# A zero-padded last product and two later starts in the attention heads of a hybrid decoder layer

## The chip, the cores and the metric

The kernel runs on one core of one Trainium2 chip. The metric is the device time of one execution in microseconds (us), as the median of several runs. TensorE is called PE in the views of the profile (PEld is its weight loads), VectorE DVE, ScalarE ACT, GpSimd POOL, SyncE SP.

## The reference, cut to what matters

One decoder layer on 512 tokens with 16 learned meta tokens ahead of them (L = 528), width 2048. A combined input projection gives q, k, v for 8 heads of 128 columns and the operands of a short convolution; after both groups come an output projection and a SwiGLU feed-forward part. The change lies in the attention heads:

```
q = rmsnorm(q per head, g_q);  k = rmsnorm(k per head, g_k)
z = q k^T / sqrt(128)
log_keep = where(key < query, log_sigmoid(-z), 0)
log_pass = reverse cumulative sum of log_keep over the keys - log_keep
w = where(key < query, exp(log_sigmoid(z) + log_pass), 0)
o = w v
```

Keys are taken in blocks of 128: four whole blocks and a last one of 16 keys (positions 512 to 527), which only the last 16 queries see, so that their weights are a 16 x 16 triangle.

## The kernel before

Activations are kept transposed, with channels on the 128 partitions and tokens along the columns. Products in float32 are made of three products of split operands (hi times hi, hi times lo, lo times hi); ACT casts the hi part and DVE subtracts it for the lo part, for weights (`split_quad`, L188 and L189, into `s_buf`) and for activations (`split`, L300 and L301) alike. The small products of the last two key blocks are plain float32, and the trace shows two PE instructions for each of them.

Each head has three large products of 16 k tiles each: pk, pq and pv. A k tile is six matmuls of 264 columns for pk and pv, and three of 512 columns for pq. The attention of a head is put in between the k tiles of the products that come after, by a list written out by hand: `after(n, work)` issues `work` when n more k tiles have been issued (`tick`). For a head h from 1 to 6 the order on PE is:

- pk of head h: nothing of its own; 8 k tiles later (in pq) the sums of squares of k (`ss_k`, L475 and L476, in `finish` of `qk_norm`).
- pq of head h; 9 k tiles later (in pv) the sums of squares of q (`ss_q`). ACT takes the squares and a scaled copy out of pq (L467, L468), splits the squares (`sh_q`, `sl_q`), and only then can L475 and L476 run.
- pv of head h; 6 k tiles later, in pk of head h+1, `attend`: v's transposes (`va`, `vb`, L522, L523), `v32` (v of the last 128 + 16 keys in plain float32), the scores z (L537 to L543), then softplus terms on ACT, DVE and POOL.
- 14 k tiles later (k tile 4 of pq of head h+1) `sums(2)`, the cumulative sums over the last keys (L592 to L595); 6 k tiles later (10 of pq) `sums(1)`; 6 later (16 of pq, its last) `sums(0)` (both L597 and L598). From the result of one, row 0 of the next one's operand is made: L603 on DVE, then a split on ACT and DVE into `sph` and `spl`. Each also takes its sums off `lb` (L606), takes the exponential (L607), sets what lies past the diagonal to zero on POOL (`causal`, L555), and splits the weights into `wh` and `wl`.
- 11 k tiles after `sums(0)` (k tile 11 of pv) `mix`, the product with v: nine split matmuls (L622 to L624), then L625 for 128 keys and L626 for the last 16. Its result is scaled and split into `st_a` (L629, L630), stored by a DMA on POOL's queue (L446), and its squares are added on POOL.

In heads 0 and 7 the distances are others already: 7 between the sums, and 12 for q in head 0. The scheduler keeps this order on PE. On ACT and DVE the instructions stand in the queue in which the scheduler put them, and each engine runs its own in order. In L626 both operands have 16 partitions, `v32[:16, P:]` and `lw[:16, 1328:1344]`; L543, the score of the same 16 keys, is a product of 128 partitions, 16 columns wide, because `kn` is padded with zeros to 640 columns. After `causal`, columns 1328 to 1343 of `lw` are zero in partitions 16 to 127 too.

Of the kernel before, what the change touches and what calls it, by code (L numbers as in the profile page):

```python
# [9 lines left out]
F32 = mybir.dt.float32  # L10
# [5 lines left out]
P = 128  # L16
D = 2048
SEQ = 512
# [15 lines left out]
def hybrid_layer(ctx: ExitStack, tc: tile.TileContext, xT, w_in, w_out, w_gu, w_down, vecs, out):  # L34
# [373 lines left out]
    kns = [apool.tile([P, 640], F32, name=f"kn{i}") for i in range(1)]  # L408
    for t in kns:
        gp.memset(t[:, L:640], 0.0)  # L410
    acc_c = accpool.tile([P, SEQ], F32, name="acc_c")
    acc_a = accpool.tile([P, SEQ], F32, name="acc_a")

# [76 lines left out]
    def head(h):  # L490

        if h:
            pk = pp.tile([P, 2, 512], F32, tag="pp", name=f"pk{h}")
            product([(pk[:, 0, :H], 0, H), (pk[:, 1, :H], H, L)], n_hl)
        else:
            pk = pk0
        kn = kns[0]
        kh = apool.tile([P, 384], F32R, tag="kh", name=f"kh{h}")
        kl = apool.tile([P, 384], F32R, tag="kl", name=f"kl{h}")
        after(8 if h else 11, qk_norm(halves(pk, H), g_k, L, kn[:, :L], (kh, kl, 384), f"k{h}"))  # L500

        if h:
            pq = pp.tile([P, 2, 512], F32, tag="pp", name=f"pq{h}")
            product([(pq[:, 0, :], META, L)], n_hl)
        else:
            pq = pq0
        qn = apool.tile([P, SEQ], F32, tag="qn", name=f"qn{h}")
        qh = apool.tile([P, SEQ], F32R, tag="qh", name=f"qh{h}")
        ql = apool.tile([P, SEQ], F32R, tag="ql", name=f"ql{h}")
        after(9 if h else 12, qk_norm(pq[:, 0, :], gq_s, SEQ, qn, (qh, ql, SEQ), f"q{h}"))  # L510

        pv = pp.tile([P, 2, 512], F32, tag="pp", name=f"pv{h}")
        product([(pv[:, 0, :H], 0, H), (pv[:, 1, :H], H, L)], n_hl)
        vt = t512(L, "e", 2)
        ve.tensor_tensor(two(vt[:, :L]), halves(pv, H), two(r), ALU.mult)
        after(6 if h else 12, lambda: attend(h, kn, kh, kl, qn, qh, ql, vt))

    def attend(h, kn, kh, kl, qn, qh, ql, vt):

        ta, tb = small(f"va{h}"), small(f"vb{h}")  # L520
        for b in range(4):
            pe.transpose(ta[:, b * P : (b + 1) * P], vt[:, b * P : (b + 1) * P], ident)  # L522
        pe.transpose(tb[:16, :P], vt[:, 512:L], ident)  # L523
        vh = apool.tile([P, 384], F32R, tag="vh", name=f"vh{h}")
        vl = apool.tile([P, 384], F32R, tag="vl", name=f"vl{h}")
        v32 = apool.tile([P, 256], F32, tag="v32", name=f"v32{h}")
        split(vh, vl, ta[:, :384])
        ve.tensor_copy(v32[:, :P], ta[:, 384:512])
        ve.tensor_copy(v32[:16, P:], tb[:16, :P])


        zs = []
        for b in range(3):
            z = small(f"z{h}_{b}")
            kk, q0 = slice(b * P, (b + 1) * P), Q0[b]
            n = SEQ - q0
            pe.matmul(z[:, :n], kh[:, kk], qh[:, q0:], start=True, stop=False)  # L537
            pe.matmul(z[:, :n], kh[:, kk], ql[:, q0:], start=False, stop=False)
            pe.matmul(z[:, :n], kl[:, kk], qh[:, q0:], start=False, stop=True)
            zs.append(z)  # L540
        z = zs[2]
        pe.matmul(z[:, 272:416], kn[:, 384:512], qn[:, 368:], start=True, stop=True)
        pe.matmul(z[:, 416:432], kn[:, 512:640], qn[:, 496:], start=True, stop=True)  # L543


        lw = apool.tile([P, 1344], F32, tag="lw", name=f"lw{h}")
        sp = apool.tile([P, 1344], F32, tag="sp", name=f"sp{h}")
        lb = apool.tile([P, 1344], F32, tag="lb", name=f"lb{h}")

        def causal(t, s):  # L550

            regions = {0: [(0, 112, 16)], 1: [(0, P, 0)], 2: [(0, P, 0), (272, 400, 0), (416, 432, 0)]}
            for a, b, base in regions[s]:
                v = t[:, SEG[s][0] + a : SEG[s][0] + b]
                gp.affine_select(  # L555
                    out=v, in_=v, pattern=[[1, b - a]], compare_op=ALU.is_gt, fill=0.0,
                    base=base, channel_multiplier=-1,
                )

        hl, ws = [None] * 3, [None] * 3  # L560
        for s in (2, 1, 0):
            a, b = SEG[s]
            z = zs[s][:, : b - a]
            sc.activation(lw[:, a:b], z, AF.Abs)
            sc.activation(lw[:, a:b], lw[:, a:b], AF.Exp, scale=-1.0)
            sc.activation(lw[:, a:b], lw[:, a:b], AF.Ln, bias=one[:, 0:1])
            ve.scalar_tensor_tensor(sp[:, a:b], z, 0.0, lw[:, a:b], ALU.max, ALU.add)
            ve.scalar_tensor_tensor(lb[:, a:b], z, 0.0, lw[:, a:b], ALU.min, ALU.subtract)
            causal(sp, s)
            th = apool.tile([P, b - a], F32R, tag=f"th{s}", name=f"sph{h}_{s}")  # L570
            tl = apool.tile([P, b - a], F32R, tag=f"tl{s}", name=f"spl{h}_{s}")
            split(th, tl, sp[:, a:b])
            hl[s] = (th, tl)
            if s == 2:

                late = lw[:, a : a + 288]
                ve.tensor_copy(late[:, :P], sp[:, 1184:1312])
                ve.tensor_tensor(late[:, P:144], sp[:, 1312:1328], sp[:, 1328:1344], ALU.add)
                gp.memset(late[:, 144:272], 0.0)
                ve.tensor_copy(late[:, 272:], sp[:, 1328:1344])  # L580
                bh = apool.tile([P, 288], F32R, tag="bh", name=f"bh{h}")
                bl = apool.tile([P, 288], F32R, tag="bl", name=f"bl{h}")
                split(bh, bl, late)
            else:
                gp.memset(lw[0:1, a : a + Q0[s + 1] - Q0[s]], 0.0)

        def sums(s):
            a, b = SEG[s]
            th, tl = hl[s]
            c = small(f"c{h}_{s}")  # L590
            if s == 2:
                pe.matmul(c[:, :432], later_r, th, start=True, stop=False)  # L592
                pe.matmul(c[:, :432], later_r, tl, start=False, stop=False)
                pe.matmul(c[:, P:416], ones_r, bh, start=False, stop=False)
                pe.matmul(c[:, P:416], ones_r, bl, start=False, stop=True)  # L595
            else:
                pe.matmul(c[:, : b - a], carry, th, start=True, stop=False)  # L597
                pe.matmul(c[:, : b - a], carry, tl, start=False, stop=True)  # L598
            if s:

                n, (a0, b0) = SEQ - Q0[s], SEG[s - 1]
                th, tl = hl[s - 1]
                ve.tensor_tensor(lw[0:1, b0 - n : b0], c[0:1, :n], sp[0:1, a : a + n], ALU.add)  # L603
                split(th[0:1, :], tl[0:1, :], lw[0:1, a0:b0])
                after(6 if 0 < h < HEADS - 1 else 7, lambda: sums(s - 1))
            ve.tensor_tensor(lb[:, a:b], lb[:, a:b], c[:, : b - a], ALU.subtract)  # L606
            sc.activation(lw[:, a:b], lb[:, a:b], AF.Exp)  # L607
            causal(lw, s)
            n = (512, 400, 272)[s]
            th = apool.tile([P, b - a], F32R, tag=f"th{s}", name=f"wh{h}_{s}")  # L610
            tl = apool.tile([P, b - a], F32R, tag=f"tl{s}", name=f"wl{h}_{s}")
            split(th[:, :n], tl[:, :n], lw[:, a : a + n])
            ws[s] = (th[:, :n], tl[:, :n])
            if s == 0:
                after(11, lambda: mix(ws))

        def mix(ws):
            o = small(f"o{h}")
            for b in range(3):
                kk, q0 = slice(b * P, (b + 1) * P), Q0[b]  # L620
                th, tl = ws[b]
                pe.matmul(o[:, q0:], vh[:, kk], th, start=b == 0, stop=False)  # L622
                pe.matmul(o[:, q0:], vh[:, kk], tl, start=False, stop=False)
                pe.matmul(o[:, q0:], vl[:, kk], th, start=False, stop=False)  # L624
            pe.matmul(o[:, Q0[3] :], v32[:, :P], lw[:, 1184:1328], start=False, stop=False)  # L625
            pe.matmul(o[:, Q0[4] :], v32[:16, P:], lw[:16, 1328:1344], start=False, stop=True)  # L626
            g = g_att[:, h : h + 1]
            oh, ol, store = stage_out(f"a{h}")
            sc.activation(oh, o, AF.Copy, scale=g)  # L629
            ve.scalar_tensor_tensor(ol, o, g, oh.bitcast(F32), ALU.mult, ALU.subtract)  # L630
            store()
            square_sum(acc_a, o, h == 0)

        after(14, lambda: sums(2))
# [624 lines left out]
```

## Time and profile before

| | |
|---|---|
| median of 3 runs | 2032.34 us (2031.63 to 2036.96) |
| the profiled execution: span, first to last instruction | 2030.6 us |
| time around the span: lowest run less the span | 1.0 us (median run less the span 1.7 us) |
| busy of the span: PE, DVE, ACT, POOL | 100%, 85%, 52%, 19% |
| the part with the attention of heads 1 to 6 (attend of head 1 to attend of head 7) | about 91 to 343 us |

The profiled execution's own device time is not listed apart from the three runs; its span is listed. The matmuls are pipelined, and their ends are modelled, so a PE that shows as busy can still hold short waits: these show in the distance from one matmul's start to the next one's, and in the idle time of the weight loads ahead of them.

### The profile page before, as it was taken

To read this page: it belongs to the slowest core of one execution; us is meant where nothing else is said; L and a number is where in the kernel's file an instruction comes from. 1 tells how busy PE (TensorE), PEld (TensorE's weight loads), DVE (VectorE), ACT (ScalarE), POOL (GpSimd) and SP (SyncE) were. 2 spreads that over 40 slices of the span, in tenths; PEclk is the share of its full clock that TensorE was granted. 3 is DMA by queue.
4 is the path that set the end of the run, shared out by engine and by line. 5 is a ranking of instruction groups with operands and counts; after the bars stand their busy time and mean duration, and the time that the engine had idled before them with its cause. 6 is when DMAs were issued, how large, how long until landed. Compare 5 with 4: busy or idle time off the path is not lost.

```text
span 2030.6 us, 39733 instructions
## 1 busy us (share of the span) xinstructions
PE 2024.3 (100%) x16158; PEld 1961.7 (97%) x16158; DVE 1720.3 (85%) x2202; ACT 1050.1 (52%) x1517; POOL 381.1 (19%) x532
## 2 busy tenths in 40 slices
PE   9999999999999999999999999999999999999999
PEld 8999999999998889999999999999999999999999
DVE  8788877588976779989989989989989989888887
ACT  7666666444444435555555555555555544444443
POOL 0111111220015440111110110110110252222111
PEclk9999999999999999999999999999999999999999
DMA  6243344753366557555555555555555999989864
GB/s 232 84 147 117 123 135 137 252 154 106 105 213 183 186 174 238 169 161 172 166 161 152 166 161 152 166 161 153 166 161 152 292 327 287 245 234 271 226 149 89
DMA packets 162279, 361.70 MB, mean 178 GB/s; under 512 B 13616, under 2 KB 74032, under 8 KB 162096
## 3 DMA queue, kind: packets, MB, share of 16 engines
q1 hardware_dynamic: 79744, 229.47, 35.4%
q0 software_dynamic: 82208, 129.65, 24.4%
q8 instruction: 127, 2.08, 0.4%
q14 instruction: 56, 0.46, 0.1%
q10 hardware_dynamic: 144, 0.04, 0.0%
HBM read 278.50 MB, written 80.61 MB: 177 GB/s over the span
## 4 chain that ended last, share of the span: by engine, by line
PE 97%; DVE 1%; ACT 1%; issue 0%; DMA 0%; POOL 0%; SPq 0%; DVEq 0%; ACTq 0%
PE x L754 40%; PE z L754 20%; PE y L754 10%; PE po L860 3%; PE po L861 3%; PE po L862 3%; PE pv L286 1%; PE pv L288 1%; PE pv L290 1%; PE pq L288 1%; PE pq L290 1%; PE pq L286 1%; PE pk L286 1%; PE pk L288 1%; PE pk L290 1%; PE pcu L286 1%
## 5 line engine op out<-in xcount | busy, mean ns | idle before, releaser
L188 ACT CAST s_buf<-w_buf 128x1024 fp32r<-128x1024 f32 (+2 forms) x665 | 659.3, 991 | 747.7 <-PE x L754 370.7
L189 DVE TENSOR_TENSOR s_buf<-w_buf,s_buf 128x1024 fp32r<-128x1024 f32 (+2 forms) x665 | 766.5, 1153 | 121.2 <-ACT s_buf L188 119.1
L754 PE MATMUL x<-f,s_buf 128*128 128x256 f32 x4224 | 500.4, 275 | 0.0
L754 PEld LDWEIGHTS x<-f,s_buf 128*128 128x128 f32 x4224 | 488.8, 188 | 0.2
L207 DVE TENSOR_TENSOR w_buf<-w_buf 128x1024 f32<-128x1024 f32 (+1 forms) x243 | 278.3, 1145 | 18.5 <-DMA w_buf<-w_in 11.8
L754 PE MATMUL z<-f,s_buf 128*128 128x256 f32 x2112 | 253.6, 275 | 0.0
L754 PEld LDWEIGHTS z<-f,s_buf 128*128 128x128 f32 x2112 | 245.9, 188 | 0.0
L1056 POOL DMA_DIRECT2D fd<-s x147 | 103.9, 919 | 701.9 <-DVE s L301 701.1
L754 PE MATMUL x<-ring,s_buf 128*128 128x256 f32 x1824 | 219.2, 275 | 0.0
L754 PEld LDWEIGHTS x<-ring,s_buf 128*128 128x128 f32 x1824 | 212.5, 188 | 0.0
L754 PE MATMUL y<-f,s_buf 128*128 128x256 f32 x1056 | 126.8, 275 | 0.0
L754 PEld LDWEIGHTS y<-f,s_buf 128*128 128x128 f32 x1056 | 123.1, 188 | 0.1
L1129 POOL DMA_DIRECT2D out_T<-d x62 | 60.8, 1012 | 284.5 <-DVE d L1137 231.8
L754 PE MATMUL z<-ring,s_buf 128*128 128x256 f32 x864 | 105.7, 275 | 0.0
L754 PEld LDWEIGHTS z<-ring,s_buf 128*128 128x128 f32 x864 | 101.5, 188 | 0.0
L225 DVE TENSOR_TENSOR w_buf<-w_buf 128x1024 f32<-128x1024 f32 (+1 forms) x81 | 92.2, 1139 | 0.0
L754 PE MATMUL x<-nh,s_buf 128*128 128x260 f32 x432 | 58.9, 282 | 0.0
L790 DVE SCALAR_TENSOR_TENSOR gu<-z,sides 128x256 f32<-128x256 f32 x44 | 18.7, 425 | 42.7 <-PE z L754 40.8
L754 PEld LDWEIGHTS x<-nh,s_buf 128*128 128x128 f32 x432 | 54.5, 188 | 0.1
L754 PE MATMUL z<-blk,s_buf 128*128 128x260 f32 x432 | 54.6, 282 | 0.0
L286 PE MATMUL pk<-nh,s_buf 128*128 128x264 f32 x256 | 52.6, 287 | 0.5 <-ACT nh L358 0.5
L754 PEld LDWEIGHTS z<-blk,s_buf 128*128 128x128 f32 x432 | 52.9, 188 | 0.0
(344 smaller groups left out, 3318.3 us busy)
## 6 DMA issues: line engine op xcount, KB each, us to landing
w_buf<-w_gu SPq DMA_DIRECT2D x176, 512.0 KB, 3.5
w_buf<-w_in SPq DMA_DIRECT2D x92, 512.0 KB, 3.4
fd<-s POOLq DMA_DIRECT2D x147, 256.0 KB, 5.3
w_buf<-w_down SPq DMA_DIRECT2D x96, 384.0 KB, 4.9
ring<-fd POOLq DMA_DIRECT2D x42, 768.0 KB, 9.0
w_buf<-w_out SPq DMA_DIRECT2D x32, 512.0 KB, 3.5
out_T<-d POOLq DMA_DIRECT2D x62, 256.0 KB, 5.6
fc<-st SPq DMA_DIRECT2D x8, 1040.0 KB, 6.3
```

The source lines that it names most:

```text
L188: sc.copy(hi, src)
L189: in_turn(ve.tensor_tensor(lo, src, hi.bitcast(F32), ALU.subtract), turn)
L207: in_turn(ve.tensor_tensor(sums[name], a, b, ALU.add), turn)
L225: ve.tensor_tensor(sums["t2"], sums["t2"], b["21"], ALU.add)
L286: pe.matmul(ps, wh, ah[:, a:b], start=k == 0, stop=False)
L288: pe.matmul(ps, wh, al[:, a:b], start=False, stop=False)
L290: pe.matmul(ps, wl, ah[:, a:b], start=False, stop=k == last)
L754: pe.matmul(p, wt[:, kk], act(part, k), start=first, stop=wt is lo and k == n - 1, skip_group_check=skip)
L860: pe.matmul(ps, hi[:, kk], ah, start=k == order[0], stop=False)
L861: pe.matmul(ps, hi[:, kk], al, start=False, stop=False)
L862: pe.matmul(ps, lo[:, kk], ah, start=False, stop=k == order[-1])
L1056: gp.dma_start(fd[c][s][:, :, k], t[:, :, i])
```

## The change

The product of the last 16 keys with v takes 128 rows: `v32` becomes one tile for all heads, whose second half is set to zero once, and L626 reads all partitions of it and of `lw`. q's sums of squares come 10 k tiles after the end of pq, one k tile later than before, in heads 1 to 7. The sums over keys are seven k tiles apart in all heads, where they were six in heads 1 to 6; `sums(1)` so comes one k tile later, `sums(0)` and `mix` two.

```diff
     for t in kns:
         gp.memset(t[:, L:640], 0.0)
+    v32 = apool.tile([P, 256], F32, name="v32")
+    gp.memset(v32[:, P:], 0.0)
...
-        after(9 if h else 12, qk_norm(pq[:, 0, :], gq_s, SEQ, qn, (qh, ql, SEQ), f"q{h}"))
+        after(10 if h else 12, qk_norm(pq[:, 0, :], gq_s, SEQ, qn, (qh, ql, SEQ), f"q{h}"))
...
-        v32 = apool.tile([P, 256], F32, tag="v32", name=f"v32{h}")
         split(vh, vl, ta[:, :384])
         ve.tensor_copy(v32[:, :P], ta[:, 384:512])
         ve.tensor_copy(v32[:16, P:], tb[:16, :P])
...
-                after(6 if 0 < h < HEADS - 1 else 7, lambda: sums(s - 1))
+                after(7, lambda: sums(s - 1))
...
-            pe.matmul(o[:, Q0[4] :], v32[:16, P:], lw[:16, 1328:1344], start=False, stop=True)
+            pe.matmul(o[:, Q0[4] :], v32[:, P:], lw[:, 1328:1344], start=False, stop=True)
```

## Rows read from the trace of the kernel before

**Rows 1.** First part of the page: the span; busy time, share and instructions of each engine.

```profile
span 2030.6 us, 39733 instructions
PE 2024.3 (100%) x16158; PEld 1961.7 (97%) x16158; DVE 1720.3 (85%) x2202; ACT 1050.1 (52%) x1517; POOL 381.1 (19%) x532
```

**Rows 2.** PE's timeline at `mix`, us 250: start, us taken, line, out<-in, count.

```profile
250.18 0.41 PE L625 MATMUL o<-lw,v 128*128 128x144 f32 x2
250.51 0.39 PE L626 MATMUL o<-lw,v 16*128 16x16 f32 x2
250.84 0.51 PE L286 MATMUL pv<-nh,s_buf 128*128 128x264 f32 x2
251.18 0.40 PE L288 MATMUL pv<-nl,s_buf 128*128 128x264 f32 x2
```

**Rows 3.** PE's timeline at the end of the scores in `attend`, us 219.

```profile
219.00 0.41 PE L542 MATMUL z<-qn,kn 128*128 128x144 f32 x2
219.24 0.29 PE L543 MATMUL z<-qn,kn 128*128 128x16 f32 x2
219.38 0.49 PE L286 MATMUL pk<-nh,s_buf 128*128 128x264 f32 x2
219.71 0.41 PE L288 MATMUL pk<-nl,s_buf 128*128 128x264 f32 x2
```

**Rows 4.** Timeline of PE's weight loads in the same two stretches.

```profile
219.12 0.31 PEld L543 LDWEIGHTS z<-qn,kn 128*128 128x128 f32 x2
...
250.51 0.29 PEld L626 LDWEIGHTS o<-lw,v 16*128 16x128 f32 x2
```

**Rows 5.** PE's timeline at `sums(0)`: first (head 1) and last (head 6) of six.

```profile
113.58 0.40 PE L597 MATMUL c<-sph,carry 128*128 128x512 f32 x1
113.82 0.39 PE L598 MATMUL c<-spl,carry 128*128 128x512 f32 x1
114.05 0.40 PE L286 MATMUL pv<-nh,s_buf 128*128 128x264 f32 x2
...
323.42 0.40 PE L597 MATMUL c<-sph,carry 128*128 128x512 f32 x1
323.87 0.50 PE L598 MATMUL c<-spl,carry 128*128 128x512 f32 x1
324.21 0.40 PE L286 MATMUL pv<-nh,s_buf 128*128 128x264 f32 x2
```

**Rows 6.** PE's timeline at the last `ss_q`, us 330.

```profile
330.69 0.40 PE L475 MATMUL ss_q<-sh_q,ones_r 128*128 128x512 f32 x1
331.00 0.50 PE L476 MATMUL ss_q<-sl_q,ones_r 128*128 128x512 f32 x1
331.34 0.41 PE L286 MATMUL pv<-nh,s_buf 128*128 128x264 f32 x2
```

**Rows 7.** Lines L598 and L476, us 80 to 350: idle before, its end, us, times.

```profile
  DVE spl L301: 1.8, 5
...
  DVE sl_q L301: 1.2, 5
```

**Rows 8.** DVE's timeline ahead of the last `sums(0)`.

```profile
320.35 1.23 DVE L189 TENSOR_TENSOR s_buf<-w_buf,s_buf 128x1024 fp32r<-128x1024 f32 x1 [0.16 <-ACT s_buf L188]
...
321.84 0.55 DVE L603 TENSOR_TENSOR lw<-c,sp 1x400 f32<-1x400 f32 x1
...
323.14 0.68 DVE L301 TENSOR_TENSOR spl<-lw,sph 1x512 fp32r<-1x512 f32 x1
```

**Rows 9.** ACT's timeline behind a `sums(0)` that started at 281.4, and its idle time.

```profile
285.82 0.62 ACT L300 CAST wh<-lw 128x512 fp32r<-128x512 f32 x1 [0.64 <-POOL lw L555]
286.35 0.59 ACT L467 ACTIVATE tmp<-pq 128x512 f32<-128x512 f32 x1
```

**Rows 10.** DVE's and PE's timelines behind head 1's `sums(0)`: `wl`, and `mix`.

```profile
120.31 0.69 DVE L301 TENSOR_TENSOR wl<-lw,wh 128x512 fp32r<-128x512 f32 x1
...
122.47 0.39 PE L622 MATMUL o<-wh,vh 128*128 128x512 f32 x1
```

## The prediction

> **What bounds the kernel now.** I read the page first. PE is busy for 2024.3 of 2030.6 us and its weight loads for 97% of the span, while DVE has 15% to spare and ACT almost half [rows 1]. So no other engine sets the end by the sum of its work, and an edit pays only where it shortens what PE spends from one matmul's start to the next one's start. As ends of matmuls are modelled, the share alone says nothing on short waits; the list of waits gives PE almost none. The next views are therefore PE's timeline around the three places that the change touches, read by the distances between starts, and then the idle time of the weight loads by line, which counts such waits. In these views the reader is to see that the product of 16 rows takes far longer than its 16 columns, and that two small products stop in the same place in most heads, each time for a lo part that DVE has just finished.
>
> **The product of 16 rows.** From the start of L625 to the start of the second k tile part behind it (L288) pass 251.18 - 250.18 = 1.00 us [rows 2]. The scores hold the same sequence with the padded form: two instructions of 144 columns, two of 16 columns with 128 partitions, then the same large product; from L542 to L288 pass 219.71 - 219.00 = 0.71 us [rows 3]. The difference is 0.29 us, there are 8 heads, and PE is never idle around it: 2.3 us. Both ends: rounding makes it 2.4 at most. If only the stretch from L626 to the large product gets shorter, 0.84 - 0.51 = 0.33 becomes 0.38 - 0.24 = 0.14 us, or 0.19 a head and 1.5 us in all. I take 2.3, since the two sequences agree instruction by instruction. The number of instructions stays at two a head. Reading 128 rows in place of 16 has no price that a row shows: the two loads of 128 rows stand 0.31 us apart from start to end, those of 16 rows 0.29 us [rows 4].
>
> The Trainium skill has a rule that speaks against this edit: "TensorE: Matmul & The Clock Gate", Part 3 (what overlaps and what doesn't), says that a weight load overlaps with matmuls in flight only when it goes to another group of rows. By that rule a padded load, which takes all rows, would have to stand in line behind L625, the edit would give nothing, and the sum would be 1.9 us instead of 4.2. The trace doesn't agree: the 128-row loads of L543 start at 219.12 [rows 4], while L542 runs from 219.00 to 219.41 [rows 3]; it is the 16-row load, at 250.51 [rows 4], that starts only with its own matmul [rows 2].
>
> Besides, the edit adds one memset, on an engine that is busy for 19% of the span [rows 1], before any head runs; I cost it at nothing, and were it exposed in full it would cost about what the mean instruction there does, 381.1 / 532 = 0.7 us [rows 1], once. The copies into `v32` waited for the product of the head before already, since the tile had one buffer; no wait is new.
>
> **The sums over keys.** In the last of the six heads, `sums(0)` takes from L597 to the next large product 324.21 - 323.42 = 0.79 us, in the first 114.05 - 113.58 = 0.47 us [rows 5]. So 0.32 us are lost in the last, none in the first. The loads' idle time says whom L598 waited for: DVE's `spl`, five times, 1.8 us in all [rows 7]. DVE's timeline shows why it is late: `spl` runs at 323.14 to 323.82, behind L603 at 321.84, which stands behind a split of weights of 1.23 us [rows 8]. L603 itself needs only `sums(1)`'s result, 6 k tiles ahead of `sums(0)`; one k tile of pq is three matmuls of 512 columns, about 0.23 us each (the distance from L597 to L598 or from L598 on without a wait [rows 5]), so 0.70 us, and the six 4.2 us. If `sums(1)` comes 0.7 us later, L603 still stands behind the same split, and `spl` ends at the same time; `sums(0)` comes two k tiles later, that is 0.7 us of pq and 0.72 us of pv, 1.4 in all. The wait was 0.32 us at most, so it goes, with about 1 us to spare. Mean of first and last, (0 + 0.32) / 2 = 0.16, times six heads: 1.0 us. Both ends: at least the longer distance behind the waiting matmul, 0.34 in place of 0.23 [rows 5], five times, 0.5 us; at most the 1.8 us of idle loads [rows 7], part of which lies under the matmul ahead.
>
> What moves with it: `sums(1)`'s two matmuls, L603, the split of row 0, and L606, L607, the causal step and a split behind it; the same for `sums(0)`; and `mix` with its 13 matmuls, `st_a`, the DMA on POOL's queue and the squares. On PE they swap places with k tiles and cost nothing. SP's queue isn't passed; on POOL's queue the store of `st_a` goes 1.4 us later, with nothing behind it but the addition of squares.
>
> **q's sums of squares.** From L475 to the next large product pass 331.34 - 330.69 = 0.65 us [rows 6], against 0.47 for the same pair of 512 columns without a wait [rows 5]: 0.18 us lost, five times, for `sl_q`, by the loads' idle time 1.2 us in all [rows 7]. Cause: with `sums(0)` issued on the last k tile of pq, its exponential, causal step and split stand in ACT's queue ahead of the squares of q; `wh` even waits 0.64 us for POOL, and the squares start only at 286.35 [rows 9], 5 us after `sums(0)` began. Two things now help: ss_q starts a k tile later (0.72 us), and `sums(0)` is issued after the copy of pq, so that the squares come out first. Either is more than the wait. I take 5 times 0.18, 0.9 us; at least 5 times 0.11 = 0.5, at most 1.2.
>
> **The sum.** 2.3 + 1.0 + 0.9 = 4.2 us, with both ends at 1.5 + 0.5 + 0.5 = 2.5 and 2.4 + 1.8 + 1.2 = 5.4. Against the profiled execution's span of 2030.6 that is 2026.4. The median of the runs lies 1.7 us above that span, the lowest run 1.0, so the median would be 2028.1 us, 2026.9 to 2029.8 by the ends. A measurement of this kernel tells about 0.3% (6.1 us) from no change, so even the whole gain, 0.2%, lies within that.
>
> **What is late next.** `mix` needs `wl` of `sums(0)`. Head 1 shows that chain where nothing else waited: from L597 at 113.58 [rows 5] to the end of `wl` at 121.00 are 7.4 us, and `mix` starts at 122.47 [rows 10], 8.9 us after L597. The distance of 11 k tiles is kept, so 1.5 us are left over; in the other heads three operations of about 0.6 us for q move from behind `wh` to ahead of it. It should just fit, and `attend` of the next head, now 9 k tiles behind `mix` and some 0.6 us earlier (0.29 + 0.16 + 0.18), is the next place to look at.
>
> **Rivals.** (a) The waits move instead of going: q's operations ahead of `wl`, or DVE's leftovers at `attend`, make PE stop for as long as was won. For it: 1.5 us of spare time against 1.8 us of moved ACT work. Against it: in head 1 neither `spl` nor `mix` waited. Then only the padding pays: 2032.3 - 2.3 = 2030.0 us. (b) The padding doesn't do what the scores suggest, as by the rule above: 2032.3 - 1.9 = 2030.4 us. The same 0.71 us sequence in the scores speaks against it. (c) The other side: `mix` waits for more than was won. It decides from the point where `wl` comes 2.2 us later than in head 1 (1.5 spare, 0.7 for 4.2 us spread over six heads). Two more splits of weights ahead of it on DVE, 1.23 us each [rows 8], would do it: a wait of 2.5 - 1.5 = 1.0 us and 0.11 behind it, six times, 6.7 us, less 4.2: 2034.8 us. Against it: PE uses up a weight tile only every 8 k tiles, so two in a row in that stretch would be unusual.
>
> **How the numbers follow.** The forecast, all three terms: 0.68. Rival (a) 0.14, (b) 0.06, (c) 0.04; the rest, 0.08, for terms at their upper ends together with a median nearer to its lowest run, and for what I don't see. The range from 2025.8 to 2031.2 holds the forecast with its ends, (a) and (b), and about a microsecond for the median's own movement. Faster by over 0.3% (under 2026.2) needs the upper ends and a favourable median: 0.10. Slower by over 0.3% (above 2038.4) needs far more than (c): 0.03. Within: 0.87.
>
> **What would show it.** L626 with 128 partitions, its two instructions nearly on top of each other, and 0.71 us from L625 to L288 in all eight heads; L598 and L476 without idle loads ahead of them, and 0.47 us for either pair; the squares of q ahead of `wh` on ACT. What would make it wrong: 1.00 us left around L626, or new idle loads at L622, L623, or at the scores.

## The result and the profile after

The changed kernel takes 2044.82 us (median of 5 runs, 2041.07 to 2045.69) against 2032.83 us for the kernel before on the same chip: a ratio over all runs of 1.0049, 95% interval 1.0037 to 1.0061 (the two medians alone lie 12.0 us, 0.6%, apart). It is slower by about half a per cent, where a gain of 0.2% was forecast. The profiled execution's span went from 2030.6 [rows 1] to 2043.7 us, 13.1 us more; it is the slowest of the five executions, so what follows accounts for the longest of them.

Lines stand one or two further on in the changed kernel: L626 and L627 are the last products of `mix` (L625 and L626 before), L598 and L599 the sums over keys, L477 and L478 the sums of squares, L479 DVE's first step behind these, L607 the subtraction from `lb`, L538 to L540 the scores, L524 and L525 v's transposes, L529 and L530 the copies of `va` and `vb` into `v32`, L631 the lo part of `st_a`.

The page hardly moves: PE is as busy as ever.

```profile
span 2043.7 us, 39735 instructions
PE 2025.0 (99%) x16158; PEld 1963.9 (96%) x16158; DVE 1716.2 (84%) x2202; ACT 1050.4 (51%) x1517; POOL 381.0 (19%) x533
```

The list of PE's waits does (line, releaser, us in total, times, longest). All three lines are new:

```profile
PE z L538 <- DVE v L530: 8.2, 5, 2.6
PE z L538 <- DVE v L529: 2.2, 1, 2.2
PE x L755 <- DVE tmp L796: 1.5, 1, 1.5
```

PE's timeline of the changed kernel, at `mix`, the third score, `sums(0)` and `ss_q`:

```profile
255.55 0.41 PE L626 MATMUL o<-lw,v 128*128 128x144 f32 x2
255.80 0.29 PE L627 MATMUL o<-lw,v 128*128 128x16 f32 x2
255.94 0.49 PE L286 MATMUL pv<-nh,s_buf 128*128 128x264 f32 x2
256.26 0.40 PE L288 MATMUL pv<-nl,s_buf 128*128 128x264 f32 x2
...
262.54 0.60 PE L524 MATMUL va<-ident,tmp 128*128 128x128 f32 x4
...
264.14 0.34 PE L540 MATMUL z<-qh,kl 128*128 128x400 f32 x1
267.05 0.59 PE L538 MATMUL z<-qh,kh 128*128 128x272 f32 x1 [2.57 <-DVE v L530]
...
333.65 0.39 PE L598 MATMUL c<-sph,carry 128*128 128x512 f32 x1
...
334.11 0.40 PE L286 MATMUL pv<-nh,s_buf 128*128 128x264 f32 x2
...
339.90 0.39 PE L477 MATMUL ss_q<-sh_q,ones_r 128*128 128x512 f32 x1
...
340.36 0.40 PE L286 MATMUL pv<-nh,s_buf 128*128 128x264 f32 x2
```

All three gains came in at their places. From L626 to the second part of the next k tile pass 256.26 - 255.55 = 0.71 us, as in the scores [rows 3], not 1.00 [rows 2]. `sums(0)` takes 0.46 us in the last of the six heads too, where it took 0.79 [rows 5], and `ss_q` 0.46 in place of 0.65 [rows 6]. What is new is the third score: from L540 to the next L538 pass 2.91 us. In heads 2 to 7 this distance is 1.55, 2.07, 2.07, 2.91, 1.35 and 2.49 us (in head 7 from the last matmul ahead of it, one of a large product that stands between), against 0.18 us in each before: 11.35 us more in all.

The third score needs a buffer. `small()` gives out four buffers of PSUM in turn; `va`, `vb` and two scores hold them, so the third score waits until DVE has copied `vb` (L530, in five heads) or `va` (L529, in head 7) out. DVE comes to that copy late. Its timeline in the changed kernel, head 5:

```profile
249.06 0.70 DVE L484 TENSOR_TENSOR kn<-tmp,tmp 128x528 f32<-128x528 f32 x1
249.68 0.68 DVE L301 TENSOR_TENSOR sl_q<-tmp,sh_q 128x512 fp32r<-128x512 f32 x1
250.29 0.68 DVE L607 TENSOR_TENSOR lb<-lb,c 128x512 f32<-128x512 f32 x1
...
252.73 0.69 DVE L301 TENSOR_TENSOR wl<-lw,wh 128x512 fp32r<-128x512 f32 x1 [1.29 <-ACT wh L300]
253.68 1.23 DVE L189 TENSOR_TENSOR s_buf<-w_buf,s_buf 128x1024 fp32r<-128x1024 f32 x1 [0.26 <-ACT s_buf L188]
254.82 0.68 DVE L479 SCALAR_TENSOR_TENSOR tmp<-ss_q,acc_x 128x512 f32<-128x512 f32 x1
...
259.51 0.69 DVE L484 TENSOR_TENSOR qn<-tmp,tmp 128x512 f32<-128x512 f32 x1
260.12 0.74 DVE L631 SCALAR_TENSOR_TENSOR st_a<-o,vec,st_a 128x512 fp32r<-128x512 f32 x1
...
265.56 1.24 DVE L301 TENSOR_TENSOR st<-x,st 128x1040 fp32r<-128x1040 f32 x1 [1.42 <-ACT st L300]
266.72 0.27 DVE L530 COPY v<-vb 16x128 f32<-16x128 f32 x1
```

The same stretch of the kernel before:

```profile
241.79 0.68 DVE L606 TENSOR_TENSOR lb<-lb,c 128x512 f32<-128x512 f32 x1
...
244.43 0.69 DVE L301 TENSOR_TENSOR wl<-lw,wh 128x512 fp32r<-128x512 f32 x1
245.04 0.70 DVE L482 TENSOR_TENSOR kn<-tmp,tmp 128x528 f32<-128x528 f32 x1
246.02 0.69 DVE L301 TENSOR_TENSOR sl_q<-tmp,sh_q 128x512 fp32r<-128x512 f32 x1 [0.27 <-ACT sh_q L300]
...
248.52 0.68 DVE L477 SCALAR_TENSOR_TENSOR tmp<-ss_q,acc_x 128x512 f32<-128x512 f32 x1
...
259.62 0.28 DVE L529 COPY v<-vb 16x128 f32<-16x128 f32 x1 [0.20 <-PE vb L523]
```

Before, `sums(0)`'s subtraction and `wl` stood ahead of `kn` and `sl_q` in DVE's queue. Now the subtraction stands behind both, so `wl` comes later, waits 1.29 us for `wh`, and holds up a split of weights and then L479, the first step behind `ss_q`. L479 starts 262.54 - 254.82 = 7.7 us ahead of `va`'s first transpose; in the same head before, L477 starts 258.88 - 248.52 = 10.4 us ahead of it (PE's timeline of before stands further down). From there to the copy of `vb` runs one chain of some 11 us through ACT and DVE: before, 259.62 - 248.52 = 11.1 us with the copy waiting for PE's `vb`; after, 266.72 - 254.82 = 11.9 us with PE waiting for the copy.

A second lateness lies in that chain. `mix` is two k tiles later, so `st_a` (L631) now stands behind `qn`, and ACT's cast into the shared buffer `st` waits until the store has landed; before, the list has no such line:

```profile
ACT st L300 <- DMA od_a<-st_a: 10.9, 6, 2.0
```

The chain of what ended last, which is nearly all PE in the heads of the kernel before, leaves PE in the changed kernel: between us 333 and 357 its largest part is the store of `st_a` (12.3%), and most of the rest is ACT, DVE and POOL. Its piece ahead of the third score of head 7:

```profile
348.31 0.76 DVE st_a L631
...
349.36 2.95 DMA od_a<-st_a
...
352.38 1.07 ACT st L300
...
353.48 1.24 DVE st L301
354.72 0.47 DVE vl L301
355.19 0.21 DVE v L529
...
355.53 0.42 PE z L538
```

PE's clock adds to it. In the windows around head 5's wait (us, busy time and count of each engine, granted clock, DMA share, GB/s) the granted clock is 0.51 of 2.4 GHz, the lower of its two levels, for 3.4 us:

```profile
262.00:267.00 5.00, 2.48 (x17) 2.00 (x16) 3.32 (x5) 2.96 (x6) 1.05 (x1) 1.00 0.62 213
267.00:270.40 3.40, 3.35 (x15) 3.36 (x16) 0.65 (x2) 1.73 (x4) 0.00 (x0) 0.51 0.71 236
```

The same happens from us 355.7, behind head 7's wait. Half speed for 3.4 us costs 1.7 us, 3.4 us for both. This is one execution: the mean granted clock of the five lies between 0.998 (here, and in one more) and 1.000 (in the one of 2042.45 us), so the drops don't come in each.

The account of the 13.1 us: 11.35 at the third scores, 3.4 for the clock, 1.7 at L755 (1.81 from one start to the next, against 0.12), 0.55 at one `ss_k` (0.79 against 0.24, us 237), less 4.3 for the three gains, is 12.7. About 0.4 us is not placed.

### The profile page after: what moved, and what is told of

Read it like the earlier page. It is cut to its first block, busy times and chain, and to the rows that moved or that the text cites. A ratio compares the mean times of both kernels' runs of the same rounds, so it can differ in the third digit from the quotient of the medians.

```text
span 2043.7 us, 39735 instructions
## 1 busy us (share of the span) xinstructions
PE 2025.0 (99%) x16158; PEld 1963.9 (96%) x16158; DVE 1716.2 (84%) x2202; ACT 1050.4 (51%) x1517; POOL 381.0 (19%) x533
## 4 chain that ended last, share of the span: by engine, by line
PE 82%; DVE 1%; ACT 1%; issue 0%; POOL 0%; DMA 0%; ACTq 0%; POOLq 0%
PE x L755 40%; PE z L755 20%; PE y L755 10%; PE po L861 3%; PE po L863 3%; PE po L862 3%; PE pcu L288 1%; PE pcu L290 1%; PE pcu L286 1%; PE pb L286 0%; PE pb L290 0%; PE pb L288 0%; DVE s_buf L189 0%; ACT s_buf L188 0%; PE po_c L863 0%
## 5 line engine op out<-in xcount | busy, mean ns | idle before, releaser
L755 PE MATMUL x<-f,s_buf 128*128 128x256 f32 x4224 | 500.5, 275 | 0.0
L755 PEld LDWEIGHTS x<-f,s_buf 128*128 128x128 f32 x4224 | 488.8, 188 | 0.2
L755 PE MATMUL z<-f,s_buf 128*128 128x256 f32 x2112 | 253.6, 275 | 0.0
L755 PEld LDWEIGHTS z<-f,s_buf 128*128 128x128 f32 x2112 | 245.9, 188 | 0.0
L755 PE MATMUL x<-ring,s_buf 128*128 128x256 f32 x1824 | 219.2, 275 | 0.0
L755 PEld LDWEIGHTS x<-ring,s_buf 128*128 128x128 f32 x1824 | 212.5, 188 | 0.0
L755 PE MATMUL y<-f,s_buf 128*128 128x256 f32 x1056 | 126.8, 275 | 0.0
L755 PEld LDWEIGHTS y<-f,s_buf 128*128 128x128 f32 x1056 | 123.1, 188 | 0.1
L755 PE MATMUL z<-ring,s_buf 128*128 128x256 f32 x864 | 105.7, 275 | 0.0
L755 PEld LDWEIGHTS z<-ring,s_buf 128*128 128x128 f32 x864 | 101.5, 188 | 0.0
L755 PE MATMUL x<-nh,s_buf 128*128 128x260 f32 x432 | 59.0, 282 | 1.5 <-DVE tmp L796 1.5
L755 PEld LDWEIGHTS x<-nh,s_buf 128*128 128x128 f32 x432 | 54.5, 188 | 1.7 <-DVE tmp L796 1.7
L755 PE MATMUL z<-blk,s_buf 128*128 128x260 f32 x432 | 54.6, 282 | 0.0
L286 PE MATMUL pv<-nh,s_buf 128*128 128x264 f32 x256 | 52.9, 287 | 0.0
```

The source lines that it names most:

```text
L286: pe.matmul(ps, wh, ah[:, a:b], start=k == 0, stop=False)
L755: pe.matmul(p, wt[:, kk], act(part, k), start=first, stop=wt is lo and k == n - 1, skip_group_check=skip)
```

## The experiments

Theory A: the late store of `st_a` alone holds up the copies. Theory B: q's chain is late, because the order on DVE behind the later sums puts L479 late, whatever `mix` does. A rival to both: `v32`, now one tile for all heads, makes something wait. The table sums up all runs; distances of the third score are for heads 2 to 7, and "to va" is the start of the first step behind `ss_q` (L479, or L477) against `va`'s first transpose, in the same heads. Ratios are to the kernel before on the same chip; spans are of one execution each and from several chips, so differences of a microsecond or two between them can be read only where the trace shows where they lie.

| run | ratio, 95% interval | span, us | distance of the third score, us | to va, us |
|---|---|---|---|---|
| before | 1 | 2030.6 | 0.18 in all | -10.4 to -10.2 |
| after | 1.0049 (1.0037 to 1.0061) | 2043.7 | 1.55, 2.07, 2.07, 2.91, 1.35, 2.49 | -9.0 to -7.7 |
| e1_pad | 0.9994 (0.9985 to 1.0003) | 2031.2 | 0.27, then 0.18 | -9.5, then -10.1 to -9.9 |
| e2_sums | 1.0040 (1.0028 to 1.0053) | 2041.4 | 0.58, 1.72, 1.78, 2.53, 0.51, 2.43 | -10.1 to -8.0 |
| e3_q | 0.9998 (0.9989 to 1.0006) | 2030.9 | 0.18 in all | -10.4, then -10.2 to -10.0 |
| e4_mix13 | 1.0004 (0.9995 to 1.0013) | 2031.9 | 0.86, 0.18, 0.18, 0.18, 1.07, 0.35 | -10.5 to -10.2 |
| e5_sp | 1.0024 (1.0014 to 1.0034) | 2035.9 | 2.76, then 0.18 | -8.7, then -10.0 to -9.5 |
| e7_mix9 | 1.0040 (1.0028 to 1.0053) | 2038.1 | 0.95 to 0.99 | -9.9, then -8.6 to -8.5 |
| e9_padq | 0.9993 (0.9985 to 1.0002) | 2027.4 | 0.18 in all | -10.2, then -9.9 |
| e10_last7 | 1.0024 (1.0015 to 1.0033) | 2035.5 | 0.61, then 0.96 to 1.12 | -8.9, then -8.6 to -8.4 |
| e11_qbehind | 1.0033 (1.0021 to 1.0046) | 2038.3 | 0.18, 1.49, 1.56, 2.45, 1.46, 2.00 | -10.35 to -8.2 |
| e12_qbehind_mix9 | 1.0028 (1.0018 to 1.0038) | 2036.5 | 0.60, then 0.97 to 1.01 | -9.2, then -8.6 |
| e13_vlate | 1.0001 (0.9992 to 1.0010) | 2031.2 | 0.33, then 0.18 | `va` itself moved |
| e14_vlate_padq | 1.0009 (1.0000 to 1.0017) | 2030.7 | 0.18 in all | `va` itself moved |

**One part at a time.** e1_pad keeps of the change the padding alone, e2_sums the later sums alone, e3_q q's sums one k tile later alone. e4_mix13 is the kernel before with `mix` two k tiles later and the sums where they were.

```diff
 e2_sums, against before
-                after(6 if 0 < h < HEADS - 1 else 7, lambda: sums(s - 1))
+                after(7, lambda: sums(s - 1))
 e4_mix13, against before
-                after(11, lambda: mix(ws))
+                after(13 if 0 < h < HEADS - 1 else 11, lambda: mix(ws))
```

> The padded product alone; q's sums and the sums over keys stand as before. My theory (the later `mix` does the harm: its result st_a is split and stored so late that ACT's cast into the same buffer `st` waits for the store, and vh and the copies out of va and vb stand behind it): no new wait at the scores, L626/L627 shorter by 0.29 us in 8 heads, 2032.8 - 2.3 = 2030.5 us. Rival 1 (the one `v32` tile for all heads makes the copies out of va and vb wait for the head before): waits of 1 to 3 us at the third score in six heads here too, some 2044 us.

> The sums over keys seven k tiles apart, alone; 16-row product and q's sums as before. My theory: the waits of L598 and L476 go (-1.9 us), and waits of 1 to 3 us at the third score come in six heads with the clock's drops behind the longest: about 2032.8 - 1.9 + 16 = 2047 us. Rival 1 (the v32 tile) and rival 2 (q's sums of squares later push DVE's chain into attend): 2031 us, no waits at the scores.

> q's sums of squares one k tile later, alone. My theory: only L476's wait goes, 2032.8 - 0.9 = 2031.9 us, no wait at the scores. Rival 2: waits at the scores of most of what after shows, 2040 us or more.

> Nothing but `mix` two k tiles later (13 instead of 11 behind sums(0), heads 1 to 6); sums, q and the 16-row product as before, so the sums' own data are as early as before. My theory: the wait at the third score comes from this alone, 2032.8 + 10 to 16 = 2043 to 2049 us. Rival 3 (it is the sums' later work on ACT and DVE, not mix's place): 2033 us, no wait at the scores.

The later sums alone give most of the loss: the median lies 8.4 us over the kernel before, the profiled span 10.8, with the same wait at the third score (8.5 us in all) and both drops of the clock. The 2047 us expected was too much. The padding and q's sums alone lose nothing and make nobody wait at the scores for more than 0.1 us, which disposes of the rival that the one `v32` tile is to blame. e4 refutes theory A as the whole cause. In it ACT waits for the landing of `st_a` longer than in the changed kernel, and the third score yet waits only twice, since L477 still comes 10.2 to 10.5 us ahead of `va`. The two views, waits of ACT and of PE, in e4_mix13:

```profile
ACT st L300 <- DMA od_a<-st_a: 12.5, 6, 2.8
```

```profile
PE z L537 <- DVE v L529: 1.2, 2, 0.7
```

e1 and e3 show something else. Padding is worth 8 times 0.30 us at `mix` by PE's starts, and yet the profiled span didn't shrink; the medians on one chip lie 1.3 us apart, not clear of noise. The distances at `sums(0)`, eight heads together, are 1.0 us longer than 0.46 each in the kernel before, and 2.7 longer in e1; two of `ss_k` are 0.8 longer together. 1.7 + 0.8 = 2.5 us of new waits in this execution for 2.4 won. Of e3's 0.9 at `ss_q`, 0.5 came back at `sums(0)` (1.5 us longer there, where it was 1.0).

**The later store, taken apart.** e5_sp writes `st_a` into `sp`, so that no cast has to wait for the landing. e7_mix9 is the changed kernel with `mix` where it stood before, in k tiles of pv. e10_last7 puts `sums(0)` alone one k tile later, together with the padding and q's sums, and keeps `mix` in its place.

```diff
 e5_sp, against after
-            oh, ol, store = stage_out(f"a{h}")
+            t = sp[:, : 2 * SEQ].bitcast(F32R).rearrange("p (a t) -> p a t", a=2)
+            oh, ol = t[:, 0], t[:, 1]
...
-            store()
+            od[f"a{h}"] = dram.tile([P, 2, SEQ], F32R, name=f"od_a{h}")
+            gp.dma_start(od[f"a{h}"], t)
 e7_mix9, against after
-                after(11, lambda: mix(ws))
+                after(9 if 0 < h < HEADS - 1 else 11, lambda: mix(ws))
 e10_last7, against after
-                after(7, lambda: sums(s - 1))
+                after(7 if s == 1 or not 0 < h < HEADS - 1 else 6, lambda: sums(s - 1))
...
-                after(11, lambda: mix(ws))
+                after(10 if 0 < h < HEADS - 1 else 11, lambda: mix(ws))
```

> The whole change, but `mix` puts its split result into the tile `sp`, which is out of use by then, instead of the buffer `st` that the convolution's blocks share; so ACT's cast into `st` waits for no store, and st's DVE step of 1.24 us moves out of the way as well. Theory A (the store's late landing holds ACT, vh and the copies behind it): no wait at the third score, before less 4 us. Theory B (q's chain on DVE, put off by the later sums(0) work, holds the copies by itself; the store adds about 1 us of it): waits of 0.3 to 0.6 us at the third score stay in most of the six heads, before less 1 to 2 us.

> The whole change, but `mix` 9 k tiles behind sums(0), which is its old place. Theory A: the store lands early, no wait at the third score; `mix` waits for wl in some heads (0.3 to 0.9 us), before less 1 to 2 us. Theory B: q's chain still begins some 2 us late, waits of 1 to 1.7 us stay at the third score: before plus 5 us.

> The padded product, q's sums a k tile later, and only sums(0) one k tile later (7 behind sums(1), which keeps its 6), `mix` at its old place (10 behind sums(0)). Theory A: no wait at the third score, 4 us less than before unless `mix` waits for wl. Theory B: the order on DVE is the question: if sums(0)'s subtraction comes behind q's split of squares, as in the whole change, waits of about 1 us at the third score and no gain; if ahead of it, 4 us less.

With `mix` back in its place (e7), `st_a` stands ahead of `qn` again and the wait for its landing is gone but for one; the third score still waits in all six heads, and in heads 3 to 7 the first step behind `ss_q` is still late (in head 2 it isn't; there the one wait for the landing that is left does it):

```profile
PE z L538 <- DVE v L530: 3.8, 6, 0.6
PE o L624 <- DVE wl L301: 1.2, 5, 0.2
```

So with the landing out of the way q's late chain still makes about 0.8 us a head at the third score (4.75 us of distance in all, head 2 included); with the store behind it, in the changed kernel, it is 11.35. This is not the whole price of the chain in e7: `mix` waits for `wl` there too, and PE's distance from `ss_q` to `va` is 0.5 to 0.9 us longer in heads 3 to 7 than the 11.2 of head 2. One k tile for `sums(0)` alone (e10) is enough for as much: 4.6 us at the third scores, with no wait for the landing of `st_a` in the list.

e5 took the wait away in heads 3 to 7, but its verdict is weak: the casts into `st` all moved early, and with them 1.24 us of DVE left the place, and the first step behind `ss_q` came early again too (-10.0 to -9.5), so it doesn't tell the landing from the step. It also missed both theories' mark: it is 5.5 us slower than the kernel before by the medians, where either expected a gain. Of that, 4.0 us stand between `sums(2)` of head 1 and that of head 2 (45.7 us, against 41.7), where the third score waits and the clock falls.

**q's squares behind `sums(0)`.** e11_qbehind takes q's squares out of pq only after `sums(0)` has been issued, so that the subtraction should come first on DVE again; e12_qbehind_mix9 is that with `mix` in its old place.

```diff
 e11_qbehind, against after
-        after(10 if h else 12, qk_norm(pq[:, 0, :], gq_s, SEQ, qn, (qh, ql, SEQ), f"q{h}"))
+        if h > 1:
+            hold = []
+            after(2, lambda: hold.append(qk_norm(pq[:, 0, :], gq_s, SEQ, qn, (qh, ql, SEQ), f"q{h}")))
+            after(10, lambda: hold[0]())
+        else:
+            after(10 if h else 12, qk_norm(pq[:, 0, :], gq_s, SEQ, qn, (qh, ql, SEQ), f"q{h}"))
```

> The whole change, but the squares, the copy and the split of q's squares are issued right behind sums(0) instead of ahead of it (heads 2 to 7); on DVE the subtraction of sums(0), L607 of the whole change, then comes ahead of the split of q's squares (0.7 us) and not behind it. Theory B (sums(0)'s work behind q's holds the split of weights, and that the first step behind ss_q on DVE, L479 there, and so the copies out of va and vb): L479 about 0.7 us earlier against attend than in the whole change, waits at the third score shorter by as much, 4 to 5 us less than the whole change. Theory A (the store of st_a, which still stands behind qn): no better than the whole change.

> The same with `mix` 9 k tiles behind sums(0), its old place, so that st_a comes ahead of qn. Theory B: waits at the third score of 0 to 0.4 us, `mix` waits less than 0.3 us, 1 to 3 us less than before. Theory A: no wait at the third score, 4 us less than before.

e11's span is 5.4 us shorter than the changed kernel's and its third scores wait 8.1 us together, not 11.35. e12 missed: its third scores still wait as e7's do, 4.5 us together. A split of weights still stands behind `wl` and ahead of L479, and the subtraction still stands behind `kn`. So the order of q's squares is only a part of it; that the rest is how late `wl` is, and what is queued behind it, is what the queues suggest and no run shows by itself.

**Without the sums.** e9_padq is the changed kernel with the sums six k tiles apart, as before.

> The padded product and q's sums a k tile later; the sums over keys as before (6 apart). Both theories: no wait at the third score, L476's wait gone, L598's stays: 2.3 + 0.9 = 3 us less than before.

It has the shortest span of all, 3.2 us under the kernel before, with no wait at the scores. But the profiled execution is the fastest of its eleven; the medians lie 1.7 us apart, of 3 expected, and its ratio doesn't stand clear of 1. It still loses 0.8 us more than the kernel before at `sums(0)`.

**Taking the need for the buffer away.** e13_vlate is the whole change, but v's transposes, their split and copies are issued 10 k tiles behind the scores, so that the third score needs no buffer that they hold. e14_vlate_padq is the same with the sums six k tiles apart.

```diff
 e13_vlate, against after
-        ta, tb = small(f"va{h}"), small(f"vb{h}")
-        for b in range(4):
-            pe.transpose(ta[:, b * P : (b + 1) * P], vt[:, b * P : (b + 1) * P], ident)
...
+        def turn_v():
+            ta, tb = small(f"va{h}"), small(f"vb{h}")
...
+        after(10, turn_v)
```

> All of the change, and the five transposes of v with the split and the two copies behind them are issued 10 k tiles behind the scores in place of ahead of them, so that the third score needs no buffer that these copies hold. Theory that the loss lies in the third score's wait for that buffer: its distances of 1.55, 2.07, 2.07, 2.91, 1.35 and 2.49 us fall to 0.18 to 0.3 (11.4 us), the granted clock doesn't drop at them (1.7 us each, twice), and the span falls from 2043.7 us to 2027 to 2030; ql still ends ahead of the first score, which comes 1.2 us earlier than in the changed kernel. Rival, that the heads are bound by the loop through ACT's and DVE's queues whichever buffer is waited for: the same wait appears at the first score, for qh or ql, or at mix, for vh or vl, of 1 us or more in most heads, and the span stays above 2036.

> The padded product, q's sums one k tile later and v's transposes 10 k tiles behind the scores, with the sums over keys six k tiles apart as before. The third score waited in no head without the later sums, so this should be within 1 us of the run with the padding and q's sums alone (span 2027.4, median 2030.5) if the late transposes cost nothing by themselves; if they cost something (vh and vl late for mix, or a wait of the transposes for a buffer), it shows here, at 1 us or more, apart from the sums.

e13's third scores stand at 0.18 us in heads 3 to 7, and 11.2 of the 11.35 us are gone; the span is 12.5 us shorter. PE's timeline in e13_vlate, head 4:

```profile
219.79 0.34 PE L544 MATMUL z<-qh,kl 128*128 128x400 f32 x1
219.97 0.28 PE L542 MATMUL z<-qh,kh 128*128 128x272 f32 x1
```

The rival, that the loop through ACT and DVE sets the pace whichever buffer is waited for, holds for one head only, head 2. There `ql` makes the first score wait, and in the profiled execution a drop of the clock follows (0.50 from us 135.0 to 138.4):

```profile
PE z L543 <- DVE ql L301: 1.3, 1, 1.3
```

From `sums(2)` of one head to that of the next, by the starts of PE, in us:

```
          head 0-1   1-2    2-3    3-4    4-5    5-6    6-7
before      37.33  41.72  41.96  42.11  42.03  42.02  42.18
after       37.04  42.95  43.47  43.48  46.38  42.76  45.56
e9_padq     37.03  41.43  41.51  41.50  41.90  41.80  41.54
e13_vlate   34.21  45.24  41.48  41.48  41.47  41.47  41.28
```

In e13 four heads in a row take 41.47 or 41.48 us, 0.55 less than the 42.03 of before: most of the 0.65 us (0.30 + 0.16 + 0.19) that the three gains are worth in such a head. Head 2's 3.5 us (45.24 against 41.72) eat it up, so the span came out above the 2027 to 2030 expected. (The 34.21 ahead of it is no gain: the first `sums(2)` of e13 starts 2.6 us later than that of before.) e14 missed its mark by more: the late transposes cost 3.3 us against e9, by the spans and by the medians. By the same distances, e14 takes 84.9 us from `sums(2)` of head 1 to that of head 3, where e9 takes 82.9, and 1.7 us more than e9 from head 7's to the end; why was not followed up.

## Why the prediction was wrong

**The three terms** were right in place and size. Padding: 8 times 0.29 forecast, 0.30 measured, 0.71 us in all eight heads but for 0.01. The Trainium skill's rule in "TensorE: Matmul & The Clock Gate", Part 3, that a load overlaps only with matmuls of another row group, doesn't hold here as it stands: PE's weight loads in the changed kernel show L627's full-height load starting at 255.68, while L626, by the modelled ends of its two matmuls, runs from 255.55 to 255.96.

```profile
255.43 0.31 PEld L626 LDWEIGHTS o<-lw,v 128*128 128x128 f32 x2
255.68 0.31 PEld L627 LDWEIGHTS o<-lw,v 128*128 128x128 f32 x2
```

Sums over keys: 1.0 forecast, 1.0 measured in the six heads. q's sums: 0.9 forecast, 0.9 measured (0.17 and four times 0.19). The sum of 4.2 us stands on PE; what the forecast lacked is a term of the other sign.

**The step that failed** is "what is late next". It priced the work that moves at nothing on PE and looked only at `mix`, which does fit: no wait of L623 or L624 is in the list. It named `attend` as the next place to look at, and didn't look; its own sign of being wrong, "new idle loads [...] at the scores", is what came. By its own numbers `attend` is 9 k tiles behind `mix`; what it left out is that q's chain, 11 us long on ACT and DVE, had only about 1 us to spare there: in head 5 the copy of `vb` waited 0.20 us for `vb` itself and ended at 259.62 + 0.28 = 259.90, and the third score came at 260.66. PE's timeline of the kernel before:

```profile
239.64 0.51 PE L598 MATMUL c<-spl,carry 128*128 128x512 f32 x1
...
246.46 0.40 PE L475 MATMUL ss_q<-sh_q,ones_r 128*128 128x512 f32 x1
246.76 0.51 PE L476 MATMUL ss_q<-sl_q,ones_r 128*128 128x512 f32 x1
...
258.88 0.60 PE L522 MATMUL va<-ident,tmp 128*128 128x128 f32 x4
...
260.66 0.28 PE L537 MATMUL z<-qh,kh 128*128 128x272 f32 x1
```

The same products in the changed kernel:

```profile
245.27 0.39 PE L599 MATMUL c<-spl,carry 128*128 128x512 f32 x1
...
251.29 0.39 PE L477 MATMUL ss_q<-sh_q,ones_r 128*128 128x512 f32 x1
251.52 0.39 PE L478 MATMUL ss_q<-sl_q,ones_r 128*128 128x512 f32 x1
```

The change moved that chain by 1.3 to 2.6 us against `va`: PE's distance from `ss_q` to `va` fell from 258.88 - 246.46 = 12.42 us to 262.54 - 251.29 = 11.25 (a k tile, the padding's gain, and the wait of `ss_q` that went), and DVE's step behind `ss_q` came 3.3 us behind L478 where it had come 1.8 us behind L476.

**"On PE they swap places with k tiles and cost nothing"** was true of PE and wrong as a price. On DVE, `sums(0)`'s subtraction came 2.15 us behind L598 before (239.64 to 241.79) and comes 5.0 us behind L599 now (245.27 to 250.29), because two other things stand ahead of it. "The squares come out first" was forecast, came true, and is the same fact: what comes out first is ahead on DVE too.

**The store of `st_a`, "with nothing behind it but the addition of squares"**, was wrong: the cast into the shared buffer behind it waits for its landing, 10.9 us in six heads. Alone that does little (e4: 12.5 us of such waits, and a ratio of 1.0004); behind the late chain it adds to it.

**The rivals.** (c) had the right sign and the wrong place: it looked for the wait at `mix`, at 1.1 us a head. (a), that DVE's leftovers at `attend` eat what was won, named the mechanism, but held that they can take no more than was won; the third scores took more than twice that, 11.35 us for 4.3. The chain that sets this wait runs on ACT and DVE, 11.1 us long before and 11.9 after, and was started later. That wins can return elsewhere is seen in e1's trace, where 2.4 us won stand against 2.5 us of new waits at `sums(0)` and `ss_k`. (b) is refuted by the 0.71 us.

**What stays open.** The scheduler's reason for the new order on DVE. The wait of 1.5 us at L755, which after, e5 and e11 have (1.2 to 1.5 us), e10 and e12 less of (0.6 and 0.4), and e2 and e13 not; there DVE's step L796 comes behind splits of weights, and no run was made on it. How the wait of 1.5 to 2.9 us in the changed kernel divides between the order on DVE, the shorter distance on PE and the landing of `st_a` is known only by parts: 4.75 us with the landing gone from five of the six heads (e7, where `mix` waits too), 4.6 without it (e10), 11.35 with it.

The Trainium skill, "Perfetto Trace Analysis", section Optimization Strategy, says that a gap which repeats on the engine that should be saturated can mean too little SBUF or PSUM for the next tile. The gap repeats in six heads, in the same place, and went when the need for the buffer did (e13). No run had a fifth buffer.

## What to carry to other kernels

Where PE's order is written out by hand, a shift by a k tile also reorders the queues of the engines that feed it: before pricing it, follow the longest chain on ACT and DVE from the shifted product to the next thing that PE needs, and write down the spare time at its end, the buffers that a copy at its end frees among it. When PE waits little because another engine's loop just fits, time won on PE comes back as waits until that loop has been shortened too. Test each part of a change alone and together with the others: here the two parts that were harmless alone came out 1.7 us under the kernel before together, though not clear of noise, and the third alone lost twice what all were worth (8.4 us by the medians, for 4.2).

## What the runs showed of the hardware

The granted clock fell in the middle of this kernel right behind waits of a few microseconds. It stood at 0.50 to 0.51 for 3.4 us behind waits of 2.57 us (us 267.0) and 2.2 us (us 355.7) in the changed kernel, and again in e2, e5, e11 and e13. In e13 the five us ahead of the drop held 3.51 us of busy PE, with a single wait of 1.3 us and smaller ones. It didn't fall behind distances of 2.07 us in heads 3 and 4, nor in e7, e10 or e12 with about 1 us. The length of the wait alone doesn't decide: in e11 the clock fell behind head 7's distance of 2.00 us and not behind head 5's of 2.45, and of the changed kernel's five executions one has a mean granted clock of 1.000. Where the clock falls, a wait of 2.5 us costs 4.2, the 1.7 us of the drop included.
